# Held weight blocks in units of the big pool: a two-layer hybrid decoder trunk on one core

## The chip, the cores and the metric

The kernel runs on one core of a Trainium2 chip. The metric is the device time of one execution in microseconds, the median of three runs. Five engines take part: TensorE (PE in the profile; its weight loads are PEld), VectorE (DVE), ScalarE (ACT), GpSimd (POOL) and the queue engine SP, which issues the DMAs.

## What is computed

Two layers of a decoder trunk on a residual stream `h` of 512 tokens by 1024 channels, all in float32:

```
for i in range(2):
    h = LN(alpha*h + 0.5*SwiGLU_a(h))             # ffa, hidden width 2816
    h = LN(alpha*h + W_o [GDN | SB | MLA](h))     # mixer, three head groups
    h = LN(alpha*h + 0.5*SwiGLU_b(h))             # ffb
    h = h + sigmoid(h W_g) * (p[i] W_p)           # per-layer input embedding (ple)
```

## The kernel before

**Splitting.** A product of float32 numbers is made from three matmuls in the type fp32r: high x high, high x low and low x high (`mm3`, lines 394 to 396; `mm2`, lines 400 to 402, does the same with high and low of one operand side by side). Every block of weights is therefore split on the chip. A block is 128 partitions by up to 1024 numbers. It is loaded into a raw place (`wraw`, three places), ScalarE casts it to the high part (`whi`, line 73, line 94 for the blocks that `add_quads` makes), and POOL or VectorE subtracts that from the raw block to get the low part (`wlo`, lines 75 and 95). `whi` and `wlo` have four places each, in the pool `wh`.

**Order of the blocks.** The class `Weights` keeps a list of all blocks of the whole program, planned before any stage by `plan_ffn`, `plan_mixer` and `plan_ple`. `next()` hands out the next block and first has the three blocks after it made as well. The instructions of all engines are put in order by a scheduler that simulates the program; an instruction can stand before others of the program text when its inputs and its places are free. A place is free when the last reader of its previous tile is done.

**Stages and held blocks.** Activations lie transposed as `x` (high and low part). A stage's output is made in two halves `n` of 512 columns and four token tiles `t` of 128 tokens. In the first half the loop over blocks is outside and the loop over tiles inside, so that a block can go after its four tiles. In the second half the last four blocks of a feed-forward (`LAST = 4`), and all four of the mixer's output and of the ple gate, are taken together, and the tile loop is outside:

```
        ws = [(W.next(), split_g(u)) for u in range(LAST)]
        ...
        for t in range(NT):
            for i, (w, g) in enumerate(ws):
                mm_u(ps1[t], t, g, w, False, i == LAST - 1)
            ln_half(t, 1, ps1[t], 2 * ALPHA)
            ln_finish(t, 4 * LN_EPS, "lnf")
            ...
            build_xT(t)
```

So tile `t` can be normalised while the matmuls of tile `t + 1` run. These four blocks are called held blocks here: each is read until the last tile. `ln_half` (lines 291 and 292) adds the matmul result to the residual on VectorE and takes statistics; `ln_finish` takes the power -0.5 on POOL (line 264, `ln_r`) and applies the norm on VectorE, ScalarE and, in the mixer, POOL (lines 302 to 308); `build_xT` transposes on PE (line 254) and splits (lines 246 and 247). In ple, `update` (lines 1214 and 1216) takes the place of the norm; its projection products `PJ` are copied out on line 1226.

**The start of a feed-forward.** Four blocks make the first two columns of hidden units, in two token halves of 256 (`part`, lines 400 to 402). After that the products follow a quad scheme with seven sums of operands: sums of weight quarters (line 92, quarters in `wq` and `wraw`) and of activations (`xf`, lines 451 and 462; `t`, lines 467 and 468).

**The big pool.** `unit` gives a tile of 128 partitions by 4 x 512 numbers from the pool `gp` with 13 places, tag `g`. Hidden activations (`g`, `gs`), `xf`, `t`, `wq`, `PT`, `PJ` and all 22 large tiles of the mixer come from it: among them `KQ0` and `KQ1`, `K`, `EU`, `SVM`, `KT`, `QT`, and the split inputs of the output product `MXh`, `MXl`, `MGh`, `MGl`. A unit has twice the size of a `whi` place.

Of the kernel before, what the change touches and what calls it, by code (L numbers as in the profile page):

```python
# [9 lines left out]
F32R = mybir.dt.float32r  # L10
# [17 lines left out]
LAST = 4  # L28
# [20 lines left out]
class Weights:  # L49
# [11 lines left out]
            self.nc.sync.dma_start(view(raw), src)  # L61
        return raw

    def pair(self):
        i = len(self.ready)
        return (self.split.tile([P, 1024], F32R, tag="whi", name=f"whi{i}"),
                self.split.tile([P, 1024], F32R, tag="wlo", name=f"wlo{i}"))

    def add(self, width, parts, eng=None, halves=False):
        def make():  # L70
            raw = self.load(parts)
            hi, lo = self.pair()
            self.nc.scalar.copy(hi[:, :width], raw[:, :width])  # L73
            for c in (slice(0, width // 2), slice(width // 2, width)) if halves else (slice(0, width),):
                (eng or self.nc.gpsimd).tensor_tensor(out=lo[:, c], in0=raw[:, c], in1=hi[:, c].bitcast(F32), op=ALU.subtract)  # L75
            return hi, lo
        self.blocks.append(make)
# [34 lines left out]
def trunk(  # L112
# [7 lines left out]
    V, G, A, T = nc.vector, nc.gpsimd, nc.scalar, nc.tensor  # L120

    opt, EN, CP = {}, {}, {}
# [24 lines left out]
    def nm(s):  # L147
        uid[0] += 1
        return f"{s}_{uid[0]}"
# [19 lines left out]
    def unit(s, dt=F32):  # L169
        return gp.tile([P, 4, 512], dt, tag="g", name=nm(s))  # L170
# [140 lines left out]
    W = Weights(nc, wr, wh, 3)  # L311

    def v3(k, n, o=0, w=None):
        w = n if w is None else w
        return lambda r: r[:, :k * n].rearrange("p (k n) -> p k n", k=k)[:, :, o:o + w]

    def rows(w, l, k0, nk, c0, c1):
        return w[l, k0 * P:(k0 + nk) * P, c0:c1].rearrange("(k p) c -> p k c", p=P)

    def plan_ffn(l, w_in, w_out):  # L320
        def tile_in(f):
            return [[(lambda r, j=j: r.rearrange("p (j k c) -> p j k c", k=4, j=2)[:, j],
                      rows(w_in, l, kh * 4, 4, j * D_FF + f * P, j * D_FF + (f + 1) * P)) for j in range(2)] for kh in range(2)]

        def slot(name):

            if ln_s["new"]:
                ln_s["new"], ln_s["r"] = False, 0
                ln_s["w"] = [x[:, i * 1024:(i + 1) * 1024] for x in (unit("wq").rearrange("p a b -> p (a b)") for _ in range(2)) for i in range(2)]
            if name != "raw":  # L330
                return lnp.tile([P, 1024], F32, tag="lng" if name == "s1" else "lnb", name=nm(name))
            ln_s["r"] += 1
            i = (ln_s["r"] - 1) % 7
            return ln_s["w"][i // 2] if i % 2 == 0 else None

        def quarter_rows(f, i, j):
            return rows(w_in, l, j * 4, 4, i * D_FF + f * P, i * D_FF + (f + 2) * P)

        for f in range(NC):
            for k, parts in enumerate(tile_in(f)):  # L340
                W.add(1024, parts, V if not W.blocks or (W.n == 0 and len(W.blocks) in XV) else None)
        for f in range(NC, NF, 2):
            W.add_quads({f"a{i + 1}{j + 1}": quarter_rows(f, i, j) for i in range(2) for j in range(2)}, slot,
                        lambda name: G if name in LOG else V, f == NC)
        for n in range(2):
            us = list(range(NF // 2))
            for u in us if n == 0 else us[:LAST - 1:-1] + us[:LAST]:
                W.add(1024, [(v3(2, 512), rows(w_out, l, u * 2, 2, n * 512, (n + 1) * 512))])

    def plan_cols(l, c, kind):  # L350
        W.add(1024, [(v3(8, P), rows(mix_w_in, l, 0, 8, c, c + P))], EN["w_" + kind], opt["eng"]["s_" + kind] == "V")

    def plan_mixer(l):
        def p_gates():
            for k0, nk in ((0, 3), (3, 3), (6, 2)):
                W.add(nk * 272, [(v3(nk, 272, 0, 16), rows(mix_w_in, l, k0, nk, C_AB, C_AB + 16)),
                                 (v3(nk, 272, 16, 256), rows(mix_w_in, l, k0, nk, C_SV, C_SV + 256))], EN["w_gates"], opt["eng"]["s_gates"] == "V")

        def p_lat():
            for u in range(4):  # L360
                W.add(832, [(v3(2, 416), rows(mix_w_in, l, u * 2, 2, C_MQ, C_MQ + 416))], EN["w_lat"], opt["eng"]["s_lat"] == "V")

        def p_gz(n):
            for u in range(2):
                W.add(1024, [(v3(4, 256), rows(mix_w_in, l, u * 4, 4, C_GZ + n * 256, C_GZ + (n + 1) * 256))], EN["w_gz"], opt["eng"]["s_gz"] == "V")

        plans = {"gates_in": p_gates, "lat_in": p_lat, "gz0": lambda: p_gz(0), "gz1": lambda: p_gz(1)}
        for k, c0 in (("si", C_SQ), ("k", C_GK), ("q", C_GQ), ("v", C_GV)):
            for c in range(4):
                plans[f"{k}{c}"] = lambda c=c0 + c * P, k=k: plan_cols(l, c, k)  # L370
        for st in opt["order"].split():
            if st in plans:
                plans[st]()
        for n in range(2):
            for u in opt["out"]:
                W.add(1024, [(v3(2, 512), rows(mix_w_o, l, u * 2, 2, n * 512, (n + 1) * 512))], EN[f"w_o{n}"], opt["eng"][f"s_o{n}"] == "V")

    def plan_ple(l):
        for n in range(2):
            W.add(1024, [(v3(2, 512), rows(ple_w_proj, l, 0, 2, n * 512, (n + 1) * 512))])  # L380
        for n in range(2):
            for u in range(4):
                W.add(1024, [(v3(2, 512), rows(ple_w_gate, l, u * 2, 2, n * 512, (n + 1) * 512))])

    for l in range(DEPTH):
        use(l)
        plan_ffn(l, ffa_w_in, ffa_w_out)
        plan_mixer(l)
        plan_ffn(l, ffb_w_in, ffb_w_out)
        plan_ple(l)  # L390
# [221 lines left out]
    def mixer(l):  # L612
# [414 lines left out]
        def stick(h2, kt):  # L1027
            sp = sps[h2]
            if True:
                q0 = kt * P  # L1030
                N = 512 - q0
                for hp in range(2):
                    z = one(kt % 2 == 1)
                    Rh = slice(hp * 64, hp * 64 + 64)
                    T.matmul(z[:, :N], SQK[Rh, 2 + h2, q0:q0 + P], SQK[Rh, h2, q0:512], start=True, stop=False)
                    T.matmul(z[:, 0:P], id_r, sb_neg, start=False, stop=True)
                    m, wt = SVM[:, 2 + hp, :N], KS[:, 2 + hp, :N]
                    act(m, z[:, :N], AF.Abs)
                    act(m, m, AF.Exp, scale=-1.0)
                    act(m, m, AF.Ln, bias=1.0)  # L1040
                    V.scalar_tensor_tensor(out=m, in0=z[:, :N], scalar=0.0, in1=m, op0=ALU.max, op1=ALU.add)
                    if kt:
                        v, o = {1: (spa, 0), 3: (spa, 1536), 2: (spb, 0)}[kt]
                        hi, lo = (pair(v, o + i * 2 * N, N)[:, hp, :] for i in range(2))
                    else:
                        hi, lo = spb[:, 1024 + hp * 512:1536 + hp * 512], LO[:, hp, :]
                    CP["sphi"](hi, m)
                    EN["splo"].tensor_tensor(out=lo, in0=m, in1=hi.bitcast(F32), op=ALU.subtract)
                    sp[kt, hp] = hi, lo
                    for k2 in range(3, kt - 1, -1):  # L1050
                        for i in range(2):
                            T.matmul(z[:, (k2 - kt) * P:N], neg_u if k2 == kt else neg_1, sp[k2, hp][i], start=False, stop=(k2 == kt and i == 1), skip_group_check=True)
                    act(wt, z[:, :N], AF.Exp)
                    T.matmul(z[Rh, :N], sv[:, kt, (2 * h2 + hp) * 64:(2 * h2 + hp + 1) * 64], wt, start=True, stop=True)
                    acc = KS[Rh, h2, :]
                    dst = acc if kt else SQK[Rh, h2, :]
                    CP["stq"](dst[:, q0:q0 + P], z[Rh, 0:P])
                    if kt < 3:
                        V.tensor_tensor(out=dst[:, q0 + P:], in0=z[Rh, P:N], in1=acc[:, q0 + P:], op=ALU.add)
# [225 lines left out]
```

## Time and profile before

| | us |
|---|---|
| median of 3 runs | 2378.92 (2372.44 to 2386.24) |
| profiled execution, its own time | 2387.08 |
| span of that execution, first to last instruction | 2385.4 |
| PE busy | 2279.2 |
| VectorE busy | 1386.6 |
| ScalarE busy | 1047.0 |
| POOL busy | 893.7 |

The mean clock that TensorE was granted over the span is 0.967 of full speed. Times in the rows below are microseconds from the first instruction of the profiled execution; the mean of one instruction in the page's groups is in ns.

### The profile page before, as it was taken

To read this page: it belongs to the slowest core of one execution; us is meant where nothing else is said; L and a number is where in the kernel's file an instruction comes from. 1 tells how busy PE (TensorE), PEld (TensorE's weight loads), DVE (VectorE), ACT (ScalarE), POOL (GpSimd) and SP (SyncE) were. 2 spreads that over 40 slices of the span, in tenths; PEclk is the share of its full clock that TensorE was granted. 3 is DMA by queue.
4 is the path that set the end of the run, shared out by engine and by line. 5 is a ranking of instruction groups with operands and counts; after the bars stand their busy time and mean duration, and the time that the engine had idled before them with its cause. 6 is when DMAs were issued, how large, how long until landed. Compare 5 with 4: busy or idle time off the path is not lost.

```text
span 2385.4 us, 40446 instructions
## 1 busy us (share of the span) xinstructions
PE 2279.2 (96%) x16834; PEld 2007.3 (84%) x16834; DVE 1386.6 (58%) x2027; ACT 1047.0 (44%) x1743; POOL 893.7 (37%) x491
## 2 busy tenths in 40 slices
PE   7999999998987999999989999999989879999999
PEld 7999888766876999988789998887668769999877
DVE  7877217557365777633487763265563667777244
ACT  4555414753443455622245553246434434556222
POOL 5222543433345422344352225424233364223442
PEclk9999999998988999999999999999889989999999
DMA  5333323212012133332233323241020122333321
GB/s 160 106 101 99 110 83 97 57 36 68 20 46 89 54 107 107 102 111 75 93 101 112 107 89 104 67 115 48 27 68 20 46 88 71 106 102 101 109 83 68
DMA packets 186792, 199.88 MB, mean 84 GB/s; under 512 B 10128, under 2 KB 151536, under 8 KB 186608
## 3 DMA queue, kind: packets, MB, share of 16 engines
q1 hardware_dynamic: 186608, 197.29, 27.2%
q8 instruction: 132, 2.16, 0.4%
q14 instruction: 52, 0.43, 0.1%
HBM read 195.17 MB, written 2.10 MB: 83 GB/s over the span
## 4 chain that ended last, share of the span: by engine, by line
PE 88%; DVE 8%; issue 2%; POOL 1%; ACT 0%; DMA 0%; SPq 0%; POOLq 0%; ACTq 0%; DVEq 0%
PE pi L394 6%; PE pi L396 6%; PE pi L395 6%; PE pc L401 4%; PE pc L402 4%; PE pc L400 4%; PE pa L402 3%; PE pa L400 3%; PE pa L401 3%; PE pb L401 3%; PE pb L402 3%; PE pb L400 3%; PE pc L394 3%; PE pc L396 3%; PE pc L395 3%; PE pi L402 2%
## 5 line engine op out<-in xcount | busy, mean ns | idle before, releaser
L75 POOL TENSOR_TENSOR wlo<-wraw,whi 128x1024 fp32r<-128x1024 f32 (+3 forms) x209 | 434.8, 2092 | 513.2 <-ACT whi L73 481.9
L73 ACT CAST whi<-wraw 128x1024 fp32r<-128x1024 f32 (+3 forms) x194 | 200.5, 1038 | 407.8 <-PE pa L396 163.9
L95 POOL TENSOR_TENSOR wlo<-wq,whi 128x1024 fp32r<-128x1024 f32 x48 | 121.6, 2533 | 295.5 <-ACT whi L94 266.4
L94 ACT CAST whi<-wq 128x1024 fp32r<-128x1024 f32 x116 | 121.9, 1051 | 131.5 <-issue 36.6
L95 POOL TENSOR_TENSOR wlo<-wraw,whi 128x1024 fp32r<-128x1024 f32 x32 | 83.2, 2601 | 232.9 <-ACT whi L94 184.8
L400 PE MATMUL pb<-x,whi 128*128 128x256 f32 x448 | 129.1, 291 | 2.4 <-ACT x L246 2.4
L94 ACT CAST whi<-wraw 128x1024 fp32r<-128x1024 f32 x84 | 88.3, 1051 | 97.3 <-issue 25.5
L401 PE MATMUL pb<-x,whi 128*128 128x256 f32 x448 | 130.6, 292 | 0.0
L402 PE MATMUL pb<-x,wlo 128*128 128x256 f32 x448 | 129.5, 290 | 0.0
L95 DVE TENSOR_TENSOR wlo<-wq,whi 128x1024 fp32r<-128x1024 f32 x68 | 85.7, 1260 | 71.6 <-ACT whi L94 71.6
L400 PE MATMUL pc<-x,whi 128*128 128x256 f32 x448 | 126.8, 284 | 0.0
L401 PE MATMUL pc<-x,whi 128*128 128x256 f32 x448 | 126.7, 283 | 0.0
L402 PE MATMUL pc<-x,wlo 128*128 128x256 f32 x448 | 126.6, 283 | 0.0
L94 ACT CAST whi<-s 128x1024 fp32r<-128x1024 f32 x80 | 84.0, 1050 | 66.8 <-PE pc L401 37.0
L95 DVE TENSOR_TENSOR wlo<-s,whi 128x1024 fp32r<-128x1024 f32 x80 | 109.1, 1364 | 2.2 <-ACT whi L94 2.2
L291 DVE SCALAR_TENSOR_TENSOR h<-h,pi 128x512 f32<-128x512 f32 x12 | 8.2, 685 | 171.6 <-PE pi L396 171.6
L394 PE MATMUL pi<-x,whi 128*128 128x512 f32 x256 | 104.2, 407 | 1.4 <-DVE gc L702 1.4
L396 PE MATMUL pi<-x,wlo 128*128 128x512 f32 x256 | 104.6, 409 | 0.0
L395 PE MATMUL pi<-x,whi 128*128 128x512 f32 x256 | 103.9, 406 | 0.0
L95 DVE TENSOR_TENSOR wlo<-wraw,whi 128x1024 fp32r<-128x1024 f32 x52 | 64.4, 1238 | 64.1 <-ACT whi L94 64.1
L402 PE MATMUL pi<-x,wlo 128*128 128x256 f32 x320 | 90.7, 283 | 1.2 <-POOL wlo L95 1.2
L400 PEld LDWEIGHTS pb<-x,whi 128*128 128x128 f32 x448 | 88.7, 199 | 3.7 <-ACT x L246 3.7
(523 smaller groups left out, 7771.4 us busy)
## 6 DMA issues: line engine op xcount, KB each, us to landing
wq<-in_ffa_w_in_dram SPq DMA_DIRECT2D x46, 512.0 KB, 3.8
wq<-in_ffb_w_in_dram SPq DMA_DIRECT2D x46, 512.0 KB, 3.9
wraw<-in_ffa_w_out_dram SPq DMA_DIRECT2D x44, 512.0 KB, 3.8
wraw<-in_ffb_w_out_dram SPq DMA_DIRECT2D x44, 512.0 KB, 3.6
wraw<-in_mix_w_in_dram SPq DMA_DIRECT2D x40, 512.0 KB, 3.9
wraw<-in_ffa_w_in_dram SPq DMA_DIRECT2D x34, 512.0 KB, 3.7
wraw<-in_ffb_w_in_dram SPq DMA_DIRECT2D x34, 512.0 KB, 3.6
wraw<-in_mix_w_o_dram SPq DMA_DIRECT2D x16, 512.0 KB, 3.6
```

The costliest lines, as they stand in the source:

```text
L73: self.nc.scalar.copy(hi[:, :width], raw[:, :width])
L75: (eng or self.nc.gpsimd).tensor_tensor(out=lo[:, c], in0=raw[:, c], in1=hi[:, c].bitcast(F32), op=ALU.subtract)
L94: nc.scalar.copy(hi, q[name])
L95: eng(name).tensor_tensor(out=lo, in0=q[name], in1=hi.bitcast(F32), op=ALU.subtract)
L291: V.scalar_tensor_tensor(out=hs, in0=hs, scalar=scale, in1=ps, op0=ALU.mult, op1=ALU.add)
L394: T.matmul(ps, ah, bh, start=first, stop=False)
L395: T.matmul(ps, ah, bl, start=False, stop=False)
L396: T.matmul(ps, al, bh, start=False, stop=last)
L400: T.matmul(dst, ah, bhl[:, 0], start=first, stop=False, skip_group_check=True)
L401: T.matmul(dst, ah, bhl[:, 1], start=False, stop=False, skip_group_check=True)
L402: T.matmul(dst, al, bhl[:, 0], start=False, stop=last, skip_group_check=True)
```

## The change

The held blocks take one unit of the big pool each, the first 1024 numbers for the high part and the second 1024 for the low part, in place of one `whi` and one `wlo` place. All other blocks stay in the four places. `pair` and `add` get an argument `home`, which the three planners set: in a feed-forward for the blocks `u < LAST` of the second half, in the mixer's output and in the ple gate for all four blocks of the second half. `unit` casts to fp32r by its type argument, and nothing else differs.

```
@@ -61,15 +61,19 @@
             self.nc.sync.dma_start(view(raw), src)
         return raw
 
-    def pair(self):
+    def pair(self, home=None):
         i = len(self.ready)
+        if home is not None:
+            u = home(f"w{i}", F32R).rearrange("p a b -> p (a b)")
+            return u[:, 0:1024], u[:, 1024:2048]
         return (self.split.tile([P, 1024], F32R, tag="whi", name=f"whi{i}"),
                 self.split.tile([P, 1024], F32R, tag="wlo", name=f"wlo{i}"))
 
-    def add(self, width, parts, eng=None, halves=False):
+    def add(self, width, parts, eng=None, halves=False, home=None):
+
         def make():
             raw = self.load(parts)
-            hi, lo = self.pair()
+            hi, lo = self.pair(home)
             self.nc.scalar.copy(hi[:, :width], raw[:, :width])
             for c in (slice(0, width // 2), slice(width // 2, width)) if halves else (slice(0, width),):
                 (eng or self.nc.gpsimd).tensor_tensor(out=lo[:, c], in0=raw[:, c], in1=hi[:, c].bitcast(F32), op=ALU.subtract)
@@ -345,7 +349,7 @@
         for n in range(2):
             us = list(range(NF // 2))
             for u in us if n == 0 else us[:LAST - 1:-1] + us[:LAST]:
-                W.add(1024, [(v3(2, 512), rows(w_out, l, u * 2, 2, n * 512, (n + 1) * 512))])
+                W.add(1024, [(v3(2, 512), rows(w_out, l, u * 2, 2, n * 512, (n + 1) * 512))], home=unit if n and u < LAST else None)
 
     def plan_cols(l, c, kind):
         W.add(1024, [(v3(8, P), rows(mix_w_in, l, 0, 8, c, c + P))], EN["w_" + kind], opt["eng"]["s_" + kind] == "V")
@@ -373,14 +377,14 @@
                 plans[st]()
         for n in range(2):
             for u in opt["out"]:
-                W.add(1024, [(v3(2, 512), rows(mix_w_o, l, u * 2, 2, n * 512, (n + 1) * 512))], EN[f"w_o{n}"], opt["eng"][f"s_o{n}"] == "V")
+                W.add(1024, [(v3(2, 512), rows(mix_w_o, l, u * 2, 2, n * 512, (n + 1) * 512))], EN[f"w_o{n}"], opt["eng"][f"s_o{n}"] == "V", unit if n else None)
 
     def plan_ple(l):
         for n in range(2):
             W.add(1024, [(v3(2, 512), rows(ple_w_proj, l, 0, 2, n * 512, (n + 1) * 512))])
         for n in range(2):
             for u in range(4):
-                W.add(1024, [(v3(2, 512), rows(ple_w_gate, l, u * 2, 2, n * 512, (n + 1) * 512))])
+                W.add(1024, [(v3(2, 512), rows(ple_w_gate, l, u * 2, 2, n * 512, (n + 1) * 512))], home=unit if n else None)
 
     for l in range(DEPTH):
         use(l)
```

## Rows read from the trace of the kernel before

**Rows 1.** The page: engine busy times, and the chain's shares by engine.
```profile
PE 2279.2 (96%) x16834; PEld 2007.3 (84%) x16834; DVE 1386.6 (58%) x2027; ACT 1047.0 (44%) x1743; POOL 893.7 (37%) x491
...
PE 88%; DVE 8%; issue 2%; POOL 1%; ACT 0%; DMA 0%; SPq 0%; POOLq 0%; ACTq 0%; DVEq 0%
```

**Rows 2.** Waits of PE over the span: total us, times, longest us.
```profile
PE pa L254 <- DVE x L247: 16.3, 10, 4.7
PE pa L254 <- DVE h L306: 15.2, 2, 7.7
PE pi L402 <- DVE wlo L95: 10.7, 3, 3.6
...
PE pb L394 <- DVE h L291: 5.7, 2, 2.8
```

**Rows 3.** Table of windows: length, then PE, PEld, DVE, ACT, POOL busy, PEclk.
```profile
753.70:776.00 22.30, 9.99 (x43) 8.49 (x43) 22.30 (x35) 8.10 (x11) 16.87 (x11) 0.62 0.43 134
1131.50:1142.00 10.50, 5.49 (x17) 4.05 (x17) 10.07 (x16) 2.12 (x5) 5.20 (x3) 0.67 0.74 241
1193.50:1206.00 12.50, 6.39 (x33) 5.74 (x34) 10.60 (x8) 4.28 (x7) 10.83 (x5) 0.73 0.76 238
370.70:378.00 7.30, 5.31 (x43) 5.03 (x43) 7.30 (x14) 2.75 (x5) 1.08 (x2) 1.00 0.56 145
799.00:815.00 16.00, 12.39 (x82) 12.19 (x81) 12.14 (x8) 5.29 (x9) 7.48 (x3) 0.79 0.23 70
688.90:705.00 16.10, 10.20 (x45) 7.95 (x46) 15.80 (x41) 6.90 (x15) 10.82 (x8) 0.58 0.34 102
```

**Rows 4.** Timeline of ACT, POOL and SP before the mixer's end.
```profile
718.98 1.06 ACT L73 CAST whi<-wraw 128x1024 fp32r<-128x1024 f32 x1 [2.34 <-PE pa L396]
...
745.14 2.96 ACT L73 CAST whi<-wraw 128x1024 fp32r<-128x1024 f32 x3 [9.88 <-PE pa L396]
...
754.64 4.72 POOL L75 TENSOR_TENSOR wlo<-wraw,whi 128x1024 fp32r<-128x1024 f32 x2 [1.11 <-ACT whi L73]
759.32 1.73 POOL L264 TENSOR_TENSOR ln_r<-ln_w,mhalf 128x1 f32<-128x1 f32 x2
...
565.90 97.77 SPq L61 DMA_DIRECT2D wraw<-in_mix_w_o_dram  x7
...
689.34 0.98 SPq L61 DMA_DIRECT2D wq<-in_ffb_w_in_dram  x2
```

**Rows 5.** Timeline of PE and DVE there: 62 matmuls, the first shown, then LN.
```profile
739.50 0.39 PE L394 MATMUL pi<-whi,MXh 128*128 128x512 f32 x1
...
753.33 0.39 PE L396 MATMUL pc<-whi,MXl 128*128 128x512 f32 x1
...
752.39 1.28 DVE L291 SCALAR_TENSOR_TENSOR h<-h,pb 128x512 f32<-128x512 f32 x2 [5.31 <-PE pb L396]
...
757.35 0.11 DVE L298 TENSOR_SCALAR ln_w<-ln_mv 128x1 f32<-128x1 f32 x1
757.36 2.55 DVE L305 SCALAR_TENSOR_TENSOR h<-h,ln_mv,lng 128x512 f32<-128x512 f32 x1
...
759.90 0.74 DVE L305 SCALAR_TENSOR_TENSOR h<-h,ln_mv,lng 128x512 f32<-128x512 f32 x1
```

**Rows 6.** Timeline of POOL and DVE, end of feed-forward b; POOL late in a.
```profile
1128.34 7.48 POOL L75 TENSOR_TENSOR wlo<-wraw,whi 128x1024 fp32r<-128x1024 f32 x3
...
1130.66 2.93 DVE L306 SCALAR_TENSOR_TENSOR h<-h,ln_r,lnb 128x512 f32<-128x512 f32 x1
...
347.56 2.39 POOL L75 TENSOR_TENSOR wlo<-wraw,whi 128x1024 fp32r<-128x1024 f32 x1 [3.05 <-ACT whi L73]
```

**Rows 7.** Tiles KQ, MGl, SVM: times from first to last start.
```profile
L1079 PE MATMUL pb<-state,KQ x224: 218/218/267, 641.7 to 688.7; 64*64 64x64 f32 x112
...
L247 DVE TENSOR_TENSOR MGl<-pa,MGh x4: 691/692/692, 699.7 to 713.4; 128x512 fp32r<-128x512 f32 x4
...
L814 PE MATMUL pc<-MW,SVM x80: 272/273/476, 639.2 to 733.8; 128*64 128x128 f32 x80
```

More of the change, by code (lines that the diff above doesn't have):

```diff
@@ L62, in load, with pair, add @@
         return raw
-    def pair(self):
+    def pair(self, home=None):
         i = len(self.ready)
+        if home is not None:
+            u = home(f"w{i}", F32R).rearrange("p a b -> p (a b)")
+            return u[:, 0:1024], u[:, 1024:2048]
         return (self.split.tile([P, 1024], F32R, tag="whi", name=f"whi{i}"),
                 self.split.tile([P, 1024], F32R, tag="wlo", name=f"wlo{i}"))
-    def add(self, width, parts, eng=None, halves=False):
+    def add(self, width, parts, eng=None, halves=False, home=None):
         def make():
             raw = self.load(parts)
-            hi, lo = self.pair()
+            hi, lo = self.pair(home)
             self.nc.scalar.copy(hi[:, :width], raw[:, :width])
@@ L347, in plan_ffn @@
             for u in us if n == 0 else us[:LAST - 1:-1] + us[:LAST]:
-                W.add(1024, [(v3(2, 512), rows(w_out, l, u * 2, 2, n * 512, (n + 1) * 512))])
+                W.add(1024, [(v3(2, 512), rows(w_out, l, u * 2, 2, n * 512, (n + 1) * 512))], home=unit if n and u < LAST else None)
     def plan_cols(l, c, kind):
@@ L375, in plan_mixer @@
             for u in opt["out"]:
-                W.add(1024, [(v3(2, 512), rows(mix_w_o, l, u * 2, 2, n * 512, (n + 1) * 512))], EN[f"w_o{n}"], opt["eng"][f"s_o{n}"] == "V")
+                W.add(1024, [(v3(2, 512), rows(mix_w_o, l, u * 2, 2, n * 512, (n + 1) * 512))], EN[f"w_o{n}"], opt["eng"][f"s_o{n}"] == "V", unit if n else None)
     def plan_ple(l):
@@ L382, in plan_ple @@
             for u in range(4):
-                W.add(1024, [(v3(2, 512), rows(ple_w_gate, l, u * 2, 2, n * 512, (n + 1) * 512))])
+                W.add(1024, [(v3(2, 512), rows(ple_w_gate, l, u * 2, 2, n * 512, (n + 1) * 512))], home=unit if n else None)
     for l in range(DEPTH):
```

## Prediction

> **What bounds the kernel now.** I read the page first. TensorE is busy 96% of a span of 2385.4 us, and the chain that ended last runs 88% on PE, 8% on VectorE and next to nothing on DMA [rows 1]. So a change can only win where PE stands still or runs slowly, and it loses where it adds such places. The reader should see how small the prize is: 2385.4 - 2279.2 = 106 us of idle PE in all.
>
> Then the list of PE's waits [rows 2]. The long ones are not in the middle of stages. They are transposes L254 waiting for a layer norm (h L306, 15.2 us in 2 waits) or for the split of the transposed activations (x L247, 16.3 us in 10), matmuls waiting for a bank that the layer norm has not yet read (h L291, 5.7 us in 2), and the first quad products waiting for a weight part (wlo L95, 10.7 us in 3). All lie at the seams, where one stage's last token tiles go through layer norm or update and the next stage's first weights are split.
>
> Then a table of windows over the seams [rows 3], because a wait hides half of the loss: after it the granted clock is down. PE's useful time in a window is busy time x PEclk, and the rest of the window is lost:
> - mixer to feed-forward b, 753.7 to 776: 22.3 - 9.99 x 0.62 = 16.1 us lost, VectorE busy throughout, POOL 16.9 of 22.3. Layer 2 has the same seam; two of them.
> - feed-forward b to the input-embedding stage (ple), 1131.5 to 1142: 10.5 - 5.49 x 0.67 = 6.8 us; two.
> - ple to the next feed-forward a, 1193.5 to 1206: 12.5 - 6.39 x 0.73 = 7.8 us; one.
> - feed-forward a to mixer, 370.7 to 378: 2.0 us at full clock; two.
>
> Sum in reach: 2 x 16.1 + 2 x 6.8 + 7.8 + 2 x 2.0 = 57.6 us. Two losses are next to the seams: the first quad products after the mixer, 799 to 815, 16 - 12.39 x 0.79 = 6.2 us, and the mixer's tail, 688.9 to 705, 16.1 - 10.2 x 0.58 = 10.2 us.
>
> Last, the timelines at the worst seam. The casts of the mixer's last weight blocks wait for PE to give back weight places: 718.98, and then three at 745.14 [rows 4]. They are the fourth held block and the first two of the next stage. POOL is then still splitting the next stage's blocks (754.64, 4.72 us) when layer norm asks it for its power (ln_r), which starts at 759.32 although VectorE had written its input (ln_w) by 757.46. VectorE's L305 takes 2.55 us beside that POOL operation and 0.74 us afterwards [rows 5]. So the weight work is late, and it is late in the very stretch where layer norm needs the same engines.
>
> **The change part by part.** Thirty-two blocks get a unit instead of a whi and a wlo place: four in each of four feed-forwards, four in each of two mixers and of two ple stages. Casts, subtractions, DMAs and matmuls stay the same in number, shape and engine, so the edit itself costs nothing on any engine. What moves is when the next stage's blocks find a free place: before, when the last token tile has used the held blocks; now, about four blocks earlier. The cover for that earlier work is the stretch before the seam, where POOL splits one block in 2.39 us after 3.05 us of idling [rows 6]; without that cover it would cost the 2.39 us a block that it costs now.
>
> *Mixer to feed-forward b.* From 739.50 on PE has 62 matmuls left, 0.227 us apart, to 753.6 [rows 5]. 24 of them end the first output half, six per token tile end the second. Today the fourth block comes at 745, so all four tiles end within 2 us (L291 from 752.39). With all weights there tile 0 can end at 739.5 + 30 x 0.227 = 746.3, 6.1 us earlier, and tile 1 a step later. POOL is no longer in the way of layer norm: 759.32 - 757.46 = 1.9 us, and L305 is shorter by 2.55 - 0.74 = 1.8. That is 6.1 + 1.9 + 1.8 = 9.8 us earlier for the first transposed tile, and the slow clock behind it (mean 0.62) goes in part: I take 11 us. Lower bound 3.7 (POOL's part alone), upper 16.1. What is late next is the second layer norm pair on VectorE, so the 6.2 us behind the first parts stay mostly: I take 2 (0 to 6.2).
>
> *Feed-forward b to ple.* POOL splits three blocks in 7.48 us from 1128.34, and L306 beside it takes 2.93 us [rows 6] against 0.74 for the same shape. Early splits free VectorE, and the projection matmuls, which need no layer norm, have their weights. I take 6 of 6.8 (3 to 6.8).
>
> *Ple to feed-forward a.* The same picture with L1214 and L1216 in place of layer norm; the first parts need only tokens 0 to 255, done long before. I take 6.5 of 7.8 (4 to 7.8). *Feed-forward a to mixer:* 1 of 2 (0 to 2).
>
> *What it costs.* In the mixer's tail the big pool of 13 units is nearly full: KQ is read until 688.7 and SVM until 733.8, and MGl is first written at 699.7 [rows 7]. The held blocks' casts and subtractions, which sat waiting until 719, can start as units come free there, with VectorE busy 15.8 of 16.1 us [rows 3]. Some four units come free there (after K, KQ and EU), and MGh and MGl need two, so two blocks can come early: 2 x 2.39 = 4.8 us on POOL [rows 6]. Bounds 0 and 4.8 per layer; I take 2.5, since POOL has 16.1 - 10.82 = 5.3 us idle in that window. The row on L305 shows it stretched by 1.8 us beside a POOL operation of 2.4 us [rows 4, 5]. The Trainium skill, page "SBUF — State Buffer", section "Who interferes with whom", says that VectorE with two SBUF inputs and a reading GpSimd lock each other out for a whole instruction; the trace agrees, and by it the price would be the full 4.8 us per layer, 4.6 us more in all. A DMA moves too: SP's queue is held 97.8 us by loads for these blocks and issues the next stage's wq at 689.34 [rows 4]; behind these stand ln, par and wq loads, none of which PE waits for today, so 0.
>
> Sum: 2 x 11 + 2 x 2 + 2 x 6 + 6.5 + 2 x 1 - 2 x 2.5 = 41.5 us. The profiled execution took 2387.1 us (1.7 around the span), 8.2 above the median of 2378.9. So it becomes 2345.6, and the median 2337.4.
>
> **Rivals.**
> - *Late units (slower).* No row shows who gets a freed unit first. If held blocks, ready since the loads of 565.9 to 663.7, take the units freed up to 696 ahead of MGh and MGl, then MGl's first write can move from 699.7 to the release of SVM after 733.8 [rows 7]: 34 us per layer, of which little is covered, as the output matmuls need MGl. That is 2 x 34 - 41.5 = 26 us more than now: 2405. It decides from 21 us of delay per layer on. For it: the pool is full at 688. Against it: the load of the next stage's wq is issued at 689.34 only [rows 4], though its source lies ready in DRAM from the start, so later users seem to queue behind earlier ones.
> - *VectorE was the wait.* It is busy 22.3 of 22.3 us in the worst seam [rows 3]. If layer norm, splits and sums keep it so, only POOL's part comes back: 2 x 3.7 + 2 x 3 + 4 = 17 us, 2362. Against it: much of that busy time is the stretching.
> - *It does not do what it says.* The raw places (three) or the order of loads could hold the next blocks back anyway, so that splits stay late: 0 to 5 us, 2374 to 2379. Against it: in the feed-forwards POOL and SP have slack between blocks.
>
> **How the numbers follow.** Forecast 0.62, VectorE 0.20, no effect 0.09, late units 0.09. A half per cent is 12 us, about what a measurement here tells from no change. Faster: 0.62 + 0.19 = 0.81; same 0.10; slower 0.09. The forecast's own bounds, all low and all high, are gains of 2 x 3.7 + 6 + 4 - 9.6 = 8 and 57.6 + 12.4 = 70; all at once is unlikely, so its own range is 2318 to 2356. The 8-in-10 range takes in the VectorE case: 2316 to 2364.
>
> **What would show it.** Right: the next stage's L73 casts and L75 subtractions lie before the seams; the 7.7 us wait of L254 on L306 and the 2.8 us wait on L291 are gone; L291 of the four tiles is spread over 6 us; PEclk stays near 1.00 at 755 to 775. The price would show as more POOL and longer L1113 or L247 between 685 and 710. Wrong if MGl's first write comes after 720, if L75 of the next stage still runs beside layer norm, or if the schedule inside the stages has moved by more than the seams gain.

## The result, and the profile after

The changed kernel took 2344.6 us (median of 6 runs, 2339.0 to 2352.1) against 2378.3 us (6 runs): ratio 0.9853, 95% interval 0.9834 to 0.9871, so 33.6 us or 1.5% faster. 2337 was forecast with a range of 2316 to 2364. The forecast was right in its sign and range. Three of its larger terms were mis-sized; two of them, in which a step of the reasoning failed, are the lesson of the case.

The page of the changed kernel, answering [rows 1]: busy times, and the chain's shares. The profiled execution took 2345.6 us, its span 2343.9.

```profile
PE 2265.5 (97%) x16834; PEld 1999.3 (85%) x16834; DVE 1379.9 (59%) x2027; ACT 1043.0 (44%) x1743; POOL 895.9 (38%) x491
...
PE 89%; DVE 7%; issue 2%; DMA 1%; POOL 1%; ACT 1%; SPq 0%; POOLq 0%; DVEq 0%; ACTq 0%
```

The work is the same. The rest of the span beside PE shrank from 106 to 78 us, and PE's busy time by 13.7 us for the same 16834 matmuls, at a mean granted clock of 0.976 where it was 0.967. Source lines behind the edit stand four later (L254 is now L258, L291 is L295, L805 is L809), and the moved blocks' tile is called w. PE's waits, answering [rows 2] (total us, times, longest us):

```profile
PE pa L258 <- DVE h L312: 9.4, 2, 4.7
PE pa L1166 <- POOL GZ L1133: 9.2, 2, 4.6
PE pc L811 <- DVE MW L809: 7.1, 4, 2.4
...
PE pa L258 <- DVE x L251: 6.3, 6, 2.6
...
PE pi L406 <- POOL wlo L99: 3.9, 3, 1.6
...
PE pa L258 <- DVE h L1220: 3.3, 1, 3.3
```

The 15.2 us of transposes on the layer norm are 9.4 us, behind a later operation of it (L312); the 5.7 us on the bank have left the list; the 16.3 us on the split activations are 6.3. The wait of transposes L811 of the mixer's attention pairs for VectorE's scaling of the exponentials (L809) grew from 2.7 us in 2 to 7.1 in 4. Two of the four, 2.4 us each, are at an early pair (698 us in layer 0), where the kernel before waits 1.35 us each; the other two, 0.3 and 1.9 us, are at layer 0's last pair and are new. A new row is that of transposes behind ple, which wait for an update (L1220), 3.3 us. The row of L811 in the kernel before:

```profile
PE pc L807 <- DVE MW L805: 2.7, 2, 1.3
```

The windows of [rows 3], set to the same places of the program (length, then PE, PEld, DVE, ACT, POOL busy, PEclk). In order: mixer to feed-forward b; feed-forward b to ple; ple to feed-forward a, drawn wide; feed-forward a to mixer; the first quads; and the mixer's tail in two pieces.

```profile
757.00:779.00 22.00, 16.53 (x103) 15.14 (x102) 19.67 (x30) 6.88 (x11) 13.35 (x9) 0.77 0.16 48
1117.00:1127.50 10.50, 10.50 (x56) 8.78 (x55) 9.62 (x21) 3.65 (x6) 1.85 (x2) 1.00 0.00 0
1166.00:1199.00 33.00, 27.92 (x145) 23.66 (x144) 17.07 (x23) 6.30 (x11) 4.71 (x2) 0.84 0.13 41
368.30:375.60 7.30, 7.30 (x55) 7.02 (x54) 6.76 (x15) 2.78 (x5) 0.92 (x1) 1.00 0.00 0
795.00:811.00 16.00, 13.48 (x110) 13.07 (x110) 12.97 (x8) 7.23 (x12) 10.92 (x5) 1.00 0.31 98
683.00:705.00 22.00, 14.98 (x86) 11.19 (x85) 21.34 (x47) 12.76 (x25) 17.16 (x14) 0.69 0.25 69
728.00:747.00 19.00, 15.91 (x65) 12.20 (x64) 5.35 (x10) 4.87 (x10) 7.22 (x4) 0.82 0.45 138
```

The same view of the kernel before, for ple drawn wide (from an earlier place, so longer) and for the tail's two pieces:

```profile
1166.00:1209.00 43.00, 36.87 (x185) 31.14 (x184) 26.13 (x24) 14.05 (x21) 19.14 (x8) 0.92 0.36 110
...
683.00:705.00 22.00, 15.95 (x119) 12.16 (x116) 21.34 (x59) 12.42 (x27) 15.41 (x12) 0.69 0.25 74
...
728.00:747.00 19.00, 18.66 (x90) 15.02 (x89) 6.81 (x12) 4.52 (x7) 2.86 (x3) 1.00 0.11 32
```

Loss is length less PE busy x PEclk, as in the prediction. Mixer to feed-forward b with its first quads: 16.1 + 6.2 before, now 22 - 16.53 x 0.77 = 9.3 and 16 - 13.48 = 2.5. Feed-forward b to ple: 6.8 to 0. Feed-forward a to mixer: 2.0 to 0. Behind ple: 43 - 36.87 x 0.92 = 9.1 before, 33 - 27.92 x 0.84 = 9.5 now, so nothing. The tail: 683 to 705 us 11.0 to 11.7, but 728 to 747 us 0.3 to 19 - 15.91 x 0.82 = 6.0. A gain is missing behind ple, and a cost of 6 us stands in layer 0's mixer where none was looked for.

### The profile page after: what moved, and what is told of

The parts are those of the page before. It is cut to its first block, busy times and chain, and to the rows that moved or that the text cites. A ratio compares the mean times of both kernels' runs of the same rounds, so it can differ in the third digit from the quotient of the medians.

```text
span 2343.9 us, 40415 instructions
## 1 busy us (share of the span) xinstructions
PE 2265.5 (97%) x16834; PEld 1999.3 (85%) x16834; DVE 1379.9 (59%) x2027; ACT 1043.0 (44%) x1743; POOL 895.9 (38%) x491
## 4 chain that ended last, share of the span: by engine, by line
PE 89%; DVE 7%; issue 2%; DMA 1%; POOL 1%; ACT 1%; SPq 0%; POOLq 0%; DVEq 0%; ACTq 0%
PE pi L398 6%; PE pi L400 6%; PE pi L399 6%; PE pc L406 4%; PE pc L405 4%; PE pc L404 4%; PE pa L406 3%; PE pa L405 3%; PE pa L404 3%; PE pb L405 3%; PE pb L406 3%; PE pb L404 3%; PE pc L398 2%; PE pc L399 2%; PE pc L400 2%; PE pi L406 2%
## 5 line engine op out<-in xcount | busy, mean ns | idle before, releaser
L79 POOL TENSOR_TENSOR wlo<-wraw,whi 128x1024 fp32r<-128x1024 f32 (+4 forms) x169 | 355.7, 2115 | 404.0 <-ACT whi L77 397.0
L77 ACT CAST whi<-wraw 128x1024 fp32r<-128x1024 f32 (+2 forms) x162 | 167.0, 1034 | 347.1 <-PE pa L400 176.7
L98 ACT CAST whi<-s 128x1024 fp32r<-128x1024 f32 x80 | 83.8, 1048 | 62.5 <-PE pc L405 33.6
L295 DVE SCALAR_TENSOR_TENSOR h<-h,pi 128x512 f32<-128x512 f32 x12 | 8.2, 684 | 167.3 <-PE pi L400 167.3
L406 PE MATMUL pa<-t,wlo 128*128 128x256 f32 x320 | 90.8, 284 | 1.7 <-DVE wlo L99 1.7
```

Of the source, the lines that this page charges most:

```text
L98: nc.scalar.copy(hi, q[name])
L295: V.scalar_tensor_tensor(out=hs, in0=hs, scalar=scale, in1=ps, op0=ALU.mult, op1=ALU.add)
L406: T.matmul(dst, al, bhl[:, 0], start=False, stop=last, skip_group_check=True)
```

## The experiments

Beside the medians I use lengths of stages from each kernel's one trace: times between the first starts on PE of the mixer's L650 (L654 after), of the gate transposes L1162 (L1166) and of the transposes of p (L413, L417), and on VectorE of the copy L1226 (L1230), as each kernel numbers them. "Fronts" is L650 to L1162, "tail, seam" L1162 to L413, "b to ple" L413 to L1226, each summed over both layers; "ple to mixer" runs from layer 0's L1226 to layer 1's L650, "first" is the stretch ahead of layer 0's L650.

```
kernel          median  ratio (95%)              span   first fronts  tail,seam b to ple ple to mixer
before          2378.3                           2385.4 383.4  627.5    819.1     67.4      427.8
after           2344.6  0.9853 (0.9834 0.9871)   2343.9 381.0  615.2    809.3     52.3      426.1
after_again     2343.6  0.9845 (0.9826 0.9863)   2340.8 381.1  612.3    809.1     52.3      426.1
ffn_only        2357.3  0.9906 (0.9888 0.9925)   2358.1 380.9  620.9    818.3     52.3      425.8
mixer_only      2369.8  0.9961 (0.9944 0.9979)   2364.2 384.7  613.9    807.0     67.4      430.1
ple_only        2375.4  0.9994 (0.9979 1.0009)   2372.9 384.3  615.4    817.9     67.3      427.8
hold            2334.9  0.9814 (0.9794 0.9834)   2334.6 382.7  614.3    799.8     52.3      425.6
hold_one        2337.3  0.9817 (0.9795 0.9838)   2336.8 382.5  619.1    798.8     52.3      424.2
late_split      2338.7  0.9833 (0.9811 0.9855)   2339.1 381.2  616.4    803.9     52.4      425.3
ple_gate        2334.9  0.9816 (0.9799 0.9832)   2331.6 381.8  614.1    805.2     52.3      418.3
hold_ple        2333.5  0.9808 (0.9792 0.9823)   2328.6 381.5  616.6    799.9     52.4      418.3
ple_only_gate   2376.3  0.9986 (0.9970 1.0003)   2374.5 384.7  618.9    819.5     67.2      422.6
all_three       2331.5  0.9799 (0.9782 0.9815)   2331.0 382.2  618.3    799.9     52.3      418.4
```

**One stage at a time.** `home=unit ...` is left at one of its three places and `home=None` put at the others.

```
ffn_only:    plan_ffn   home=unit if n and u < LAST else None    (mixer, ple: None)
mixer_only:  plan_mixer home=unit if n else None                 (feed-forwards, ple: None)
ple_only:    plan_ple   home=unit if n else None                 (feed-forwards, mixer: None)
```

> Units for the held blocks of the four feed-forwards alone; mixer and ple blocks in whi and wlo places as before. My theory, from the two traces: the feed-forward seams give 2 x 7 us (feed-forward b to ple) and 2 x 2.9 us (feed-forward a to mixer), so 2378.3 - 19.8 = about 2358 us; the mixer's tail and its seam stay as they were. Rival (the terms of my prediction): 2 x 6 + 2 x 1 = 14 us, 2364. Second rival: the gain comes only from all blocks together, because the places form one chain: under 8 us, over 2370.

> Units for the mixer's four held blocks alone. My theory, from the two traces: the seam behind the mixer gives 2 x 11 us and the tail ahead of it takes 2 x 7 us back, a net of about 8 us: 2370 us. Rival (the terms of my prediction): 2 x 13 - 2 x 2.5 = 21 us, 2357. In the trace: the wait of transposes on the layer norm gone, and a new wait of transposes L811 on the scaled exponentials (MW L809) in the last 20 us before the last latent product.

> Units for the held gate blocks of the two ple stages alone. My theory, from the two traces: the seam behind ple loses 8.8 us before and 9.1 us after, so nothing is won: 2378 us, within 3. Rival (the term of my prediction): 6.5 us, 2372.

Measured: 21.7 us faster, 9.2 us faster, and no difference that the interval shows. The medians' ratios take off 0.0094 + 0.0039 + 0.0006 = 0.0139 in sum and the whole change 0.0147, so the parts act apart and no chain over all places is needed. The feed-forwards' units bring the two "b to ple" stretches (67.4 to 52.3, 15.1 us), and 2.5 ("first") and 2.0 ("ple to mixer") ahead of the mixers. The mixer's units bring a net 12.1 us in "tail, seam", not the 21 of my terms; 2.3 us that this kernel spends longer behind ple I did not look into. The sizes that I read from the two traces held in all three, and the prediction's own split fell for mixer and ple. Of what I expected in the trace of the mixer's units, the new wait of L811 came; the wait on the layer norm did not go, it is 9.4 us as in the changed kernel.

**The mixer's tail: cover or contention?** The timelines of the changed kernel there. PE first (time, us, then line, operation and tiles; in brackets the idle time before and what ended it), then VectorE and POOL:

```profile
704.18 0.71 PE L398 MATMUL pb<-w,MXh 128*128 128x512 f32 x2
...
731.90 0.41 PE L811 MATMUL pc<-ident,MW 128*128 128x128 f32 x2 [0.29 <-DVE MW L809]
...
734.26 0.41 PE L811 MATMUL pc<-ident,MW 128*128 128x128 f32 x2 [1.95 <-DVE MW L809]
...
730.27 1.48 DVE L809 TENSOR_SCALAR MW<-MW,su 128x256 f32<-128x256 f32 x1
...
732.24 1.87 DVE L809 TENSOR_SCALAR MW<-MW,su 128x256 f32<-128x256 f32 x1
...
726.87 7.10 POOL L79 TENSOR_TENSOR wlo<-wraw,whi 128x1024 fp32r<-128x1024 f32 x3
```

A latent pair is two heads of the latent attention for one token tile: scores on PE, exponentials on ScalarE, their scaling L809 on VectorE, then transposes L811 and value products L818 on PE. Matmuls that PE can issue while this chain runs on the other engines are its cover, or filler. Two things happen at once. The weights of the second output half are there early, so PE issues its matmuls (pb from w) from 704 us on as filler, and after 731.6 us it has none to issue until the pair is done at 736.65; before, they started at 723.5 us and lay under the last latent pair. And POOL, with places free, splits three of the next stage's blocks beside that pair, where VectorE's L809 takes 1.48 and 1.87 us. PE then waits, and its clock stands at half from 736 to 741 us. One edit gives the cover back and leaves POOL's order up to the layer norm alone (VectorE's and ScalarE's order in the tail changes with PE's); another moves POOL and leaves the order of the other three engines alone.

```
hold:       in latent:  held[h2, qt] = T.matmul(s[R, 0:P], vm[...], pT[...], ...)
            in mm_o of the second half, at its first matmul i of each tile:
                tc.add_manual_dep(i.ins, held[1, 2].ins.name, NOSYNC)
hold_one:   the same for tiles 1 to 3 alone
late_split: subtraction L79 of the next stage's first blocks:
                tc.add_manual_dep(<its instruction>, <MXl L1140, k = 2>, NOSYNC)
```

> All units as in the changed kernel, but the first matmul of the mixer's second output half may not be issued by TensorE before the last value product of the latent pair (heads 2 and 3, tile 2), the last but one pair; nothing else is changed. My theory: the changed kernel loses some 7 us per mixer in the tail because TensorE spends the second half's matmuls (the only cover of the last latent pair) from 704 us on; held back, they cover it again, the waits of L811 on MW L809 (1.9 us) and the half clock at 735 to 742 go, and 2 x 5 to 2 x 7 us come back: 2331 to 2335 us against 2344.6. Rival: the price is that of GpSimd splitting weight blocks beside VectorE (L809 1.5 to 1.9 us instead of 0.4), which the hold does not touch: 2345, within 3.

> All units as in the changed kernel, and TensorE, VectorE and ScalarE keep their order to the instruction; GpSimd alone is told to split the next stage's first blocks (three x 2.4 us) after the mixer's last own operation (MXl L1140) instead of beside the last latent pair. It parts the two halves of the tail's price. If the price were GpSimd beside VectorE alone, the two L809 of the last pair fall from 1.5 and 1.9 us to 0.4, the wait goes and 2 x 5.5 to 2 x 7 us come back: 2331 to 2334 us against 2344.6. If it is the missing cover (TensorE has nothing else to issue), the chain of the pair is shorter by only 2.6 us and most of it still stands open: 2 x 2.6 = about 5 us, 2339 to 2340, the half clock behind it in part still there. If the moved splits collide with layer norm: 2345 or more.

> As the run that held the second half back, but tile 0's 18 matmuls (4.1 us) are free again and only tiles 1 to 3 are held. The last latent pair's chain is some 7 us from its first score product to its first transposes' use, so 4.1 us of cover leave 2 to 3 us open per mixer, while the 1.5 us wait at the pair before it goes. Cover theory: 2335 to 2339 us, between the held kernel's 2334.9 and the changed kernel's 2344.6. If any held matmul would do as well: 2335 or less.

The kernel with the held half, the same pair (timelines of PE, VectorE, POOL):

```profile
720.76 0.45 PE L398 MATMUL pb<-w,MXh 128*128 128x512 f32 x1
...
726.96 0.60 PE L811 MATMUL pc<-ident,MW 128*128 128x128 f32 x4
...
722.21 0.97 DVE L809 TENSOR_SCALAR MW<-MW,su 128x256 f32<-128x256 f32 x1
...
723.29 2.30 DVE L809 TENSOR_SCALAR MW<-MW,su 128x256 f32<-128x256 f32 x1
...
718.30 7.14 POOL L79 TENSOR_TENSOR wlo<-wraw,whi 128x1024 fp32r<-128x1024 f32 x3 [0.43 <-ACT whi L77]
```

and its window around that pair (11 us earlier than 728 to 747):

```profile
717.00:736.00 19.00, 18.67 (x91) 15.09 (x90) 5.09 (x9) 6.88 (x12) 9.29 (x5) 1.00 0.50 154
```

POOL still splits beside the pair and L809 is stretched even more (0.97 and 2.30 us), yet PE waits for nothing there (it still does at earlier pairs) and its clock stays up: the window loses 0.3 us as before the change. "Tail, seam" falls from 809.3 to 799.8 and the median to 2334.9, with all runs (2333.0 to 2336.3) below all of the changed kernel's (2337.8 and up, both series). The rival, which had the hold change nothing, falls.

The kernel with late splits: L809 is short, and the wait is shorter, not gone (timelines of VectorE and PE, then the window):

```profile
730.62 0.36 DVE L809 TENSOR_SCALAR MW<-MW,su 128x256 f32<-128x256 f32 x1
...
732.58 0.35 DVE L809 TENSOR_SCALAR MW<-MW,su 128x256 f32<-128x256 f32 x1
...
733.08 0.41 PE L811 MATMUL pc<-ident,MW 128*128 128x128 f32 x2 [0.90 <-DVE MW L809]
734.01 0.73 PE L818 MATMUL pc<-MW,SVM 128*64 128x128 f32 x8 [0.52 <-DVE MW L813]
```

```profile
728.00:747.00 19.00, 17.30 (x77) 13.79 (x76) 4.99 (x14) 4.91 (x11) 8.31 (x4) 0.91 0.43 136
```

The window still loses 19 - 17.30 x 0.91 = 3.3 of 6.0 us. How much of the rest is the late splits and how much the clock, two more traces tell: the changed kernel's second one and that of the gated kernel (described under the next heading), at the same place and with the same order of all four engines in this tail:

```profile
724.00:743.00 19.00, 15.91 (x65) 12.14 (x64) 5.37 (x10) 4.87 (x10) 7.16 (x4) 0.82 0.45 138
```

```profile
722.00:741.00 19.00, 15.91 (x77) 12.50 (x76) 7.65 (x14) 4.93 (x11) 7.59 (x4) 1.00 0.45 138
```

PE's idle time is 3.1 us in all of them, and the clock stayed up in the gated one, so one order loses 6.0 or 3.1 us (4.5 in the trace of the mixer's units alone, at 0.91). The part that the order fixes is the idle time: 3.1 us with the units, 1.7 with late splits, 0.3 held. So contention is about half of that idle time, and only because nothing covers it; the half clock behind it comes and goes. The stage and the median are no sure measure of the late splits: 809.3 - 803.9 = 5.4 us fit the cover theory, but the gated kernel, with splits as early as ever, has 805.2; and the runs (2333.7 to 2348.2, median 2338.7) overlap the changed kernel's. By the same measure the hold's 9.5 us are 805.2 - 799.8 = 5.4 where the clock fell less.

With tile 0 free again (hold_one) the median is 2337.3, where the cover theory had it, but its reason fell: PE waits 0.2 us at the last pair and not 2 to 3, and the stage is 798.8. So 4.1 us of cover less cost nothing, and that each held matmul is needed is not shown.

**Behind ple.** In ple's first half four Tanh read the gate sums, VectorE's updates follow (L1218, L1220), and the transposes wait for the updates. The changed kernel's timelines there (the last product of tile 0's gate sum on PE, then ACT, VectorE, POOL, PE):

```profile
1151.68 0.39 PE L400 MATMUL pb<-whi,x 128*128 128x512 f32 x1
...
1154.71 1.05 ACT L77 CAST whi<-wraw 128x1024 fp32r<-128x1024 f32 x1 [5.00 <-DMA wraw<-in_ffa_w_in_dram]
1155.67 0.58 ACT L183 ACTIVATE sg<-pb 128x512 f32<-128x512 f32 x1
...
1156.28 2.50 DVE L1218 SCALAR_TENSOR_TENSOR sg<-sg,PJ 128x512 f32<-128x512 f32 x1 [12.32 <-ACT sg L183]
1158.82 2.78 DVE L1220 SCALAR_TENSOR_TENSOR h<-sg,h 128x512 f32<-128x512 f32 x1
1161.52 2.88 DVE L1218 SCALAR_TENSOR_TENSOR sg<-sg,PJ 128x512 f32<-128x512 f32 x1
...
1155.84 8.02 POOL L79 TENSOR_TENSOR wlo<-wraw,whi 128x1024 fp32r<-128x1024 f32 x3 [3.66 <-ACT whi L77]
...
1172.79 1.09 PE L258 MATMUL pa<-ident,h 128*128 128x128 f32 x4 [3.27 <-DVE h L1220]
```

ScalarE sat 5.0 us before a cast of the next stage's block, waiting for that block's DMA, with the first Tanh queued behind it: it starts at 1155.67, 3.6 us after its sum was done at 1152.07. Then three instructions of the updates ran beside POOL's splits at 2.5 to 2.9 us instead of 0.69, 6.1 us more in all. In the kernel before, the first Tanh (1166.72) waits for PE alone. The edit lets only ple's own casts pass the Tanh:

```
ple_gate: casts of the next stage's blocks:
    tc.add_manual_dep(<cast L77>, <last Tanh of the first half>, NOSYNC)
```

> All units as in the changed kernel; in ple, ScalarE may cast the next stage's first blocks only after the four Tanh of the first output half. My theory of why the seam behind ple gave nothing: these casts now stand ahead of the Tanh in ScalarE's order and wait for their weights' DMA (5.0 us of idling ahead of one), so the updates begin late, beside GpSimd's three splits, and TensorE waits 3.3 us for one; with the gate 3 to 5 us come back, once: 2340 to 2342 us against 2344.6. Rival: VectorE's updates are late because GpSimd stretches them, gate or not: 2344 to 2345.

> Units for ple's held blocks alone, with the casts of the next stage behind the four Tanh. Units alone gave 2375.4 to 2377 us (ratio 0.9994). If the casts ahead of the Tanh are what ate the gain, this now shows the gain that my prediction put there, 6.5 us, and the trace has the seam's loss near 2 us: 2369 to 2372. Rival (the seam is bound by VectorE whatever the order): 2375 to 2378.

The gated kernel (timelines of ACT, VectorE, POOL, then its window for 1166 to 1199):

```profile
1143.86 0.60 ACT L183 ACTIVATE sg<-pb 128x512 f32<-128x512 f32 x1 [5.31 <-PE pb L400]
...
1148.43 2.94 ACT L77 CAST whi<-wraw 128x1024 fp32r<-128x1024 f32 x3
...
1144.49 0.69 DVE L1218 SCALAR_TENSOR_TENSOR sg<-sg,PJ 128x512 f32<-128x512 f32 x1 [8.78 <-ACT sg L183]
...
1149.55 10.68 POOL L79 TENSOR_TENSOR wlo<-wraw,whi 128x1024 fp32r<-128x1024 f32 x4 [8.53 <-ACT whi L77]
```

```profile
1153.00:1186.00 33.00, 31.10 (x192) 27.12 (x191) 20.81 (x23) 9.00 (x14) 13.37 (x6) 1.00 0.30 97
```

The Tanh now waits for PE alone, the first half's updates run at 0.69 us, the last one ending 0.4 us into POOL's next splits, and the window loses 1.9 us instead of 9.5. "Ple to mixer" falls from 426.1 to 418.3, 7.8 us, more than the 3 to 5 I expected, since the half clock behind the wait goes too. The gate takes away the late Tanh and the stretched updates together, because POOL's splits move with the casts; how the 7.8 us divide between the two is not shown. The median fell by 9.7 us against the first series of the changed kernel; the part above 7.8 is within the intervals, and in its one trace "tail, seam" is 4.1 us shorter too, most of it the clock. With ple's units alone the gate brings 427.8 to 422.6 in the trace, so 5.2 of the 6.5 us of the prediction were there to be had. The median (2376.3) does not show them: I missed there, and its interval (0.9970 to 1.0003) holds both nothing and 7 us. The gate without any units was not run.

**Together.**

> The two edits together: second half of the mixer's output held behind the last but one latent pair, and the casts behind the four Tanh. If the two losses are separate stages with nothing in common, the gains add: 2334.9 less 3 to 5, so 2330 to 2332 us. Rival, if the gate gives nothing: 2335.

> Held second half, gated casts and late splits together. The last latent pair is covered by matmuls once the half is held, so the stretched L809 costs nothing there and the late splits add nothing: 2331 to 2335, as without them (2333.5). Rival: GpSimd beside VectorE costs by itself, 2 x 2.6: 2328 to 2329. If the late splits come into the layer norm's way: 2337 or more.

> The changed kernel itself beside them, for its level on this chip and for a second trace of the same order. Three runs (held 9.7 us, gate 9.7 us, both together 11.1 us below 2344.6) do not add. If the changed kernel's level is the reason: 2338 to 2341 here. If it is 2344 to 2346 again, the two losses overlap. Tail of the mixer in the trace: the wait of L811 (4.7 us) is the same to 0.1 us, since the order fixes it; whether the clock falls to half behind it (5.7 us lost at 730 to 750 in the first trace, 2.8 in the trace of the gated kernel with the same order there) may differ.

Stage by stage the edits add: the kernel with both has 799.9 in "tail, seam" as with the hold alone and 418.3 behind ple as with the gate alone. Late splits on top change neither (799.9, 418.4), as expected once the pair is covered. The medians add less well: 2333.5 with both, above the 2330 to 2332 expected, against 2334.9 with either. The changed kernel's level is no reason (2343.6 again; its second trace has the wait of L811 again, 7.1 us, and the clock drop of layer 0's tail). Part of it is that the gated kernel's tail was already down to 805.2 by the clock, which leaves 5.3 us there for the hold and not 9.5. The fronts move by several us between kernels and hide a sum of this size; I could not resolve the rest. All three together, at 2331.5 us, ratio 0.9799, are the fastest version here, 12 us below the changed kernel in the same series.

## Why the prediction was right, and where it was not

**Feed-forward b to ple**, 2 x 6: the mechanism was right, 15.1 measured, somewhat above the bound of 2 x 6.8. The whole loss of this window went, with the feed-forwards' units alone.

**Mixer to feed-forward b**, 2 x 11 and 2 x 2: the mechanism was right. The sums L295 of the four tiles are spread over 7.0 us (751.24 to 758.27), and POOL's power for tile 0 starts when its input is there (755.38 after 755.16). But the 6.1 us by which tile 0 can end earlier were not free. From the first gate transposes to tile 0's sum it is 752.39 - 693.5 = 58.9 us before, 751.24 - 691.2 = 60.0 after, and 742.69 - 688.4 = 54.3 with the held half: the tail ate it. Gross, hold against before, it is 819.1 - 799.8 = 19.3 us for both mixers where I had 26, so this term was too large. What stays is the rival on VectorE, in part. Tile 0's layer norm now reaches from 751.24 to the end of L312, among the sums and statistics of three other tiles, and PE still waits 4.7 us:

```profile
751.24 0.69 DVE L295 SCALAR_TENSOR_TENSOR h<-h,pb 128x512 f32<-128x512 f32 x1 [0.15 <-PE pb L400]
...
762.25 1.07 DVE L312 TENSOR_TENSOR h<-h,lnb 128x512 f32<-128x512 f32 x1
...
763.38 1.97 PE L258 MATMUL pa<-ident,h 128*128 128x128 f32 x8 [4.71 <-DVE h L312]
```

PEclk near 1.00 over this seam was forecast and is wrong: 0.77.

**The price in the mixer's tail**, 2 x 2.5 with bounds 0 and 4.8: mis-sized, and looked for in the wrong place. It was put at 685 to 710 us as load on POOL and VectorE; that stretch lost only 0.7 us more. It came at 728 to 747 us, 5.7 us more in layer 0 of the changed kernel's trace (2.8 of it idle time, the rest the clock), and the hold gives 9.5 us back for both. The step that failed is that casts, subtractions, DMAs and matmuls stay the same in number, "so the edit itself costs nothing on any engine": the matmuls did stay the same, but they were the cover of the last latent pair, and weights that come early let PE spend it early.

**Ple to feed-forward a**, 6.5: the step that failed is "the same picture". The units let the next stage's casts move past the Tanh on ScalarE, in front of a DMA that was not in yet, and POOL's splits with them beside the updates. I had asked what the moved blocks wait for, and not what waits behind the moved casts. Measured nothing with units alone, 7.8 us once the casts are gated (5.2 where ple alone has units).

**Feed-forward a to mixer**, 2 x 1: 2.5 and 2.0 measured, so under-sized; this window's whole 2.0 went.

**The sum.** By stages, before to after: first -2.4, tail and seam -9.8, b to ple -15.1, ple to mixer -1.7, the rest of the span -0.2, together -29.2 us, and the fronts -12.3, which is the 41.5 of the two spans. That the forecast sum was also 41.5 is chance: the stages that it summed gave 29.2. The range was wide enough for the miss, and the fronts filled part of it. Of the fronts' 12.3 us, 8.5 - 3.4 = 5.1 are the clock drops shown below. Over all traces the 8 fronts of kernels without units in the mixer average 310.3 us and the 18 with them 307.8. Two of these, 5 us, and the 29.2 make 34, the timed difference; whether those 5 us belong to the change is open: the kernel with the feed-forwards' units alone has the changed kernel's order ahead of layer 0's tail.

**Late units** fell: MGl is first written at 698.5 us (699.7 before).

The Trainium skill, page "SBUF — State Buffer", section "Who interferes with whom", says that VectorE instructions with two SBUF inputs, and tensor_scalar in a two-port mode, contend with a reading GpSimd. The traces agree: L1218 and L1220 take 2.5 to 2.9 us for 0.69, L809 up to 2.30 for 0.36. What the chain does with it is decided by cover: held, the longer L809 cost nothing.

## What to carry to other kernels

Data that comes early lets the scheduler put an engine's filler early in its queue: before giving it room, look for the latency-bound chain that the filler covers today, and keep some back for it. When work moves forward past other instructions of its queue, look for what is now queued behind it and whether its own input is there. Read the gain stage by stage from starts of the same instructions, since the medians here carry some 4 us of other things, and within a stage part idle time, which the order fixes, from the clock behind it, which one trace has and the next has not.

## What the runs showed of the hardware

TensorE's clock fell to half in stretches in which the rows show it busy throughout, and not in each execution. Windows of the mixer's front: the changed kernel, the same kernel's second trace at the same place of the program, and the kernel before in its second layer:

```profile
462.00:472.00 10.00, 10.00 (x34) 6.92 (x33) 3.21 (x6) 7.01 (x13) 5.80 (x5) 0.66 0.16 46
```

```profile
462.00:472.00 10.00, 10.00 (x50) 6.79 (x50) 4.78 (x10) 8.40 (x18) 6.06 (x6) 1.00 0.16 47
```

```profile
1680.00:1698.00 18.00, 18.00 (x67) 11.93 (x69) 4.74 (x14) 7.70 (x17) 2.68 (x3) 0.53 0.03 8
```

PE is busy throughout, with small matmuls before and in the stretch, at a mean granted clock of 0.66, 1.00 and 0.53, so for two thirds of the first stretch and nearly all of the last at 1.2 instead of 2.4 GHz: 10 x 0.34 = 3.4, 0 and 18 x 0.47 = 8.5 us lost. The front of layer 0, whose instructions stand in one order in the nine traces of kernels with the feed-forwards' units, took 304.6 to 310.6 us. Such drops are as large as two of the terms of this prediction, and one trace alone cannot tell them from an effect.
